# One mLSTM stage of a hybrid decoder layer: maxima differences taken from the heads' banks, keys transposed in one group, state products on column tiles

## The chip, the core and the metric

The kernel runs on one core of a Trainium2 chip. Its time is what the device needs for one launch, in microseconds (us); the figure given for a kernel is the median of several runs. One further execution is recorded by the hardware profiler, and everything read from a trace below is from that one. The engines that matter here are TensorE (PE in the profile; its weight loads are listed apart as PEld), VectorE (DVE), ScalarE (ACT), GpSimd (POOL) and the queue that issues most transfers, SyncE (SP).

## The reference

The layer is x + half a SwiGLU FFN, then x + a token mixer, then x + half a second FFN, each between two RMS norms, for 512 tokens and a width of 1024. The mixer has four HGRN2 heads and four mLSTM heads; only the mLSTM part concerns us. Cut to what is computed for one chunk of one head:

```python
b = jnp.cumsum(fc, axis=-1)                       # log forget gates, summed
a = b + m[..., None]
D = jnp.where(causal, b[..., :, None] - b[..., None, :] + ic[..., None, :], -jnp.inf)
m_t = jnp.maximum(a, jnp.max(D, axis=-1))         # running maximum
inter = jnp.exp(a - m_t)
P = jnp.einsum("bhtd,bhsd->bhts", qc, kc) * jnp.exp(D - m_t[..., None])
num = inter[..., None] * jnp.einsum("bhtd,bhdv->bhtv", qc, C) + jnp.einsum("bhts,bhsv->bhtv", P, vc)
den = inter * jnp.einsum("bhtd,bhd->bht", qc, n) + jnp.sum(P, axis=-1)
h = num / jnp.maximum(jnp.abs(den), jnp.exp(-m_t))[..., None]
w = jnp.exp(b[..., -1:] - b + ic - m_t[..., -1][..., None])
C_new = inter[..., -1][..., None, None] * C + jnp.einsum("bhs,bhsd,bhsv->bhdv", w, kc, vc)
```

Queries and keys of a head have 64 channels, values 128. All inputs and the output are float32.

## The kernel before

The kernel takes chunks of 128 tokens (NT = 4 of them), not the reference's 64, and computes the running maximum for all 512 tokens in rows before the stage below. Large products are made as three fp32r products of split operands (`mm3`, lines 196 to 200: high by high, high by low, low by high); the small products of the mixer are plain float32.

In the mixer, TensorE's queue is filled by hand. The projections of the layer (HGRN2 gates, mLSTM values and so on) are generators in `self.jobs`, and `self.fill(n)` (L1124) advances them by n steps between pieces of the recurrences. While the mLSTM stage runs, a step of a projection is one `t_mm`, three fp32r products of 128x512, seen in the trace as L198, L199, L200. These are called filling products below. Each projection holds four of the eight PSUM banks while it runs; the other four rotate among everything else. Weights of the projections lie in four places; ScalarE rounds each one (L294), VectorE subtracts for the low part (L296), and a place comes free when TensorE has read it.

The mLSTM stage is `mlstm_scores` (L1645) with `mlstm_head` (L1621) and `neg_m` (L1602):

- `self.nm2` holds the negated running maxima, heads in rows, as a high part in rows 0 to 3 and a low part in rows 32 to 35. `self.sel` is a matrix of ones and zeros with six planes; the product of plane n with `nm2` (`neg_m(n)`, L1605, 36 rows, 512 columns) spreads a row over partitions into a PSUM bank. Planes 0 to 3 spread one head over all 128 partitions. Planes 4 and 5 spread a pair: the pair's first head on partitions 0 to 63, its second on 64 to 127.
- For each head, `mlstm_head` reads the spread bank on VectorE: it adds the row term (L1628), copies the chunk ends to `nend` (L1629), clamps (L1630), then ScalarE exponentiates (L1631) and GpSimd masks (L1632). The score products (L1640) take 64 rows each; two heads of a pair alternate, one on partitions 0 to 63, one on 64 to 127. L1642 multiplies scores and decays into `pT`.
- For each pair p, `mlstm_scores` then makes the spread product of the pair's plane, copies it to SBUF (L1674), subtracts each chunk's preceding end (L1677) and exponentiates (L1680): the factor of the queries. The same for chunk ends (L1682, L1685) gives the factor of the state. Three transposes (L1691) turn the keys of the pair, L1692 multiplies them with their weights into `kw`, L1698 multiplies the queries into `qdm`; `fill(3)` follows, nine filling products.
- The states: for each chunk c of three and each pair, one product (L1706) of `kw` (128 channels of both heads) with the values and a column of ones of both heads (258 columns). Its diagonal blocks are the two heads' updates; the other two blocks are not used. VectorE copies (L1716) or accumulates (L1718) the blocks into `C`, which is zero off the diagonal blocks (memset, L1669).
- `mlstm_values` (L1745) then multiplies queries with `C` (L1753) and scores with values (L1756).

Instructions stand on TensorE's queue in the order of the program here: score products, then spread product, transposes, nine filling products, the same for the second pair, four state products, six filling products, two state products.

`sel` is built on GpSimd in `masks` (L1333 to L1343), early in the mixer; its last copy is kept as `self.selected`, behind which GpSimd issues the transfers that add up sums of later weights (L944).

Of the kernel before, what the change touches and what calls it, by code (L numbers as in the profile page):

```python
# [18 lines left out]
NT = T // P  # L19
# [9 lines left out]
NH = 4  # L29
# [94 lines left out]
class Layer:  # L124
# [1187 lines left out]
    def masks(self, mc, mb):  # L1312

        nc = self.nc

        self.mask = mb.tile([P, len(LEVELS), 2, 64], I32, name="mask")
        nc.gpsimd.memset(self.mask, 1)
        for n, c in enumerate(LEVELS):
            for odd in range(2):
                m = self.mask[:, n, odd, :].rearrange("p (b c) -> p b c", c=c)  # L1320
                for sign, base in ((1, 0), (-1, c - 1)):
                    base, step = (base + sign * (P - 1), -sign) if odd else (base, sign)
                    pat = [[-2 * c * sign, 64 // c], [0, c]]
                    nc.gpsimd.affine_select(m, m, pattern=pat, compare_op=ALU.is_ge, fill=0.0, base=base, channel_multiplier=step)
        self.eye = mb.tile([P, 2, P], I32, name="eye")
        nc.gpsimd.memset(self.eye, 1)
        for odd in range(2):
            e = self.eye[:, odd, :]
            pat, base, step = ([[1, P]], 1 - P, 1) if odd else ([[1, P]], 0, -1)
            nc.gpsimd.affine_select(e, e, pattern=pat, compare_op=ALU.is_equal, fill=0.0, base=base, channel_multiplier=step)  # L1330

        sel = mb.tile([4, 6, 2, 64], F32, tag="tmp", bufs=1, name="sel")
        nc.gpsimd.memset(sel, 1.0)  # L1333
        self.sel = mc.tile([36, 6, P], F32R, name="selr")
        nc.gpsimd.memset(self.sel.bitcast(I32), 0)
        for n in range(6):
            pat = [[0, 2], [0, 64]] if n < 4 else [[-1, 2], [0, 64]]
            base = -n if n < 4 else -2 * (n - 4)
            nc.gpsimd.affine_select(
                sel[:, n], sel[:, n], pattern=pat, compare_op=ALU.is_equal, fill=0.0, base=base, channel_multiplier=1  # L1340
            )
        for r in (0, 32):
            self.selected = nc.gpsimd.tensor_copy(self.sel[r : r + 4], sel.rearrange("p n a b -> p n (a b)"))  # L1343
    def forget_gates(self, mb):

        nc = self.nc
# [274 lines left out]
    def mlstm_head(self, h):  # L1621

        nc = self.nc
        nm = self.neg_m(h)
        nm4 = nm.rearrange("p (c t) -> p c t", c=NT)
        e = self.st("e")
        e4 = e.rearrange("p (c t) -> p c t", c=NT)
        nc.vector.tensor_tensor(e4, nm4, self.aT[:, :, h : h + 1].broadcast_to([P, NT, P]), op=ALU.add)  # L1628
        nc.vector.tensor_copy(self.nend[:, h, :].rearrange("p (c o) -> p c o", o=1), nm4[:, :, P - 1 : P])  # L1629
        nc.vector.tensor_scalar(e, e, 0.0, None, op0=ALU.min)  # L1630
        nc.scalar.activation(e, e, AF.Exp)  # L1631
        nc.gpsimd.affine_select(  # L1632
            e4, e4, pattern=[[0, NT], [1, P]], compare_op=ALU.is_ge, fill=0.0, base=0, channel_multiplier=-1
        )
        yield
        o = 64 * (h % 2)
        sc = self.ps()
        for c in range(NT):
            s = slice(c * P, (c + 1) * P)
            nc.tensor.matmul(sc[:, s], self.qk[o : o + 64, 2 + h // 2, s], self.qk[o : o + 64, h // 2, s], start=True, stop=True)  # L1640
            yield
        nc.vector.scalar_tensor_tensor(self.pT[:, h, :], sc, 0.125, e, op0=ALU.mult, op1=ALU.mult)  # L1642
        yield

    def mlstm_scores(self, mc):  # L1645

        nc = self.nc
        self.nend = mc.tile([P, NH, NT], F32, name="nend")
        self.pT = mc.tile([P, NH, T], F32, name="pT")
        H = [self.mlstm_head(h) for h in range(NH)]  # L1650
# [12 lines left out]
        nc.vector.tensor_tensor(w, self.aT, self.nend.rearrange("p h c -> p c h"), op=ALU.add)  # L1663
        nc.scalar.activation(w, w, AF.Exp)
        self.qdm = mc.tile([P, 2, 3 * P], F32, name="qdm")
        self.kw = mc.tile([P, 2, 3, P], F32, name="kw")

        self.C = mc.tile([P, 2, 3, 258], F32, name="C")
        nc.gpsimd.memset(self.C, 0.0)  # L1669
        dcs = []  # L1670
        for p in range(2):
            nm = self.neg_m(4 + p)
            ns = self.st("ns")
            nc.scalar.copy(ns, nm)  # L1674
            n4 = ns.rearrange("p (c t) -> p c t", c=NT)
            d = self.st("dq", 3 * P)
            nc.vector.tensor_tensor(  # L1677
                d.rearrange("p (c t) -> p c t", c=3), n4[:, 1:, :], n4[:, :3, P - 1 : P].broadcast_to([P, 3, P]), op=ALU.subtract
            )
            nc.scalar.activation(d, d, AF.Exp)  # L1680
            dc = self.col(2)
            nc.vector.tensor_tensor(  # L1682
                dc.rearrange("p (c o) -> p c o", o=1), n4[:, 1:3, P - 1 : P], n4[:, 0:2, P - 1 : P], op=ALU.subtract
            )
            nc.scalar.activation(dc, dc, AF.Exp)  # L1685
            dcs.append(dc)
            wp = self.col(8)[:, :6]
            nc.vector.tensor_copy(wp.rearrange("p (c a) -> p c a", a=2), w[:, :3, 2 * p : 2 * p + 2])
            pt = self.ps()
            for c in range(3):  # L1690
                nc.tensor.transpose(pt[:, c * P : (c + 1) * P], self.qk[:, 2 + p, c * P : (c + 1) * P], self.ident)  # L1691
            nc.vector.tensor_tensor(  # L1692
                self.kw[:, p].rearrange("p c (a d) -> p (c a) d", a=2),
                pt[:, : 3 * P].rearrange("p (n d) -> p n d", d=64),
                wp[:, :, None].broadcast_to([P, 6, 64]),
                op=ALU.mult,
            )
            nc.vector.scalar_tensor_tensor(self.qdm[:, p, :], self.qk[:, p, P:], 0.125, d, op0=ALU.mult, op1=ALU.mult)  # L1698
            self.fill(3)
        banks = {}  # L1700
        for c in range(3):
            for p in range(2):
                if c < 2:
                    for at in ((0, p), (1, p)) if c == 0 else ((2, p),):
                        ps = banks[at] = self.ps()
                        nc.tensor.matmul(  # L1706
                            ps[:, :258], self.kw[:, p, at[0], :],
                            self.vm[:, at[0], 2 * p : 2 * p + 2, :].rearrange("p a v -> p (a v)"), start=True, stop=True,
                        )
# [12 lines left out]

# [268 lines left out]
```

## Time and profile before

| | |
|---|---|
| median of 3 runs | 921.05 us (920.13 to 921.39) |
| profiled execution, its own time | 920.66 us |
| its span in the trace | 918.9 us |
| TensorE clock granted, mean | 0.998 |
| busy: PE, DVE, ACT, POOL | 99%, 84%, 57%, 21% of the span |
| mean busy share of the DMA engines by slice | between a tenth and nine tenths |

How to read it: the span is cut from the first to the last instruction of the trace; the launch adds 1.8 us. A row of the trace in order of time gives start, duration, engine, line, operation, output and inputs, shapes (output, input), and how many instructions were merged; in brackets, how long the engine was idle before and what ended that. A float32 product appears as two records (two passes), an fp32r product or a transpose as one. Matmuls are pipelined, so their durations overlap and the distance of two starts is what one costs. "Waits" lists who waited for whom: total, times, longest.

### The profile page before, as it was taken

To read this page: it belongs to the slowest core of one execution; us is meant where nothing else is said; L and a number is where in the kernel's file an instruction comes from. 1 tells how busy PE (TensorE), PEld (TensorE's weight loads), DVE (VectorE), ACT (ScalarE), POOL (GpSimd) and SP (SyncE) were. 2 spreads that over 40 slices of the span, in tenths; PEclk is the share of its full clock that TensorE was granted. 3 is DMA by queue.
4 is the path that set the end of the run, shared out by engine and by line. 5 is a ranking of instruction groups with operands and counts; after the bars stand their busy time and mean duration, and the time that the engine had idled before them with its cause. 6 is when DMAs were issued, how large, how long until landed. Compare 5 with 4: busy or idle time off the path is not lost.

```text
span 918.9 us, 18150 instructions
## 1 busy us (share of the span) xinstructions
PE 910.2 (99%) x7332; PEld 877.3 (95%) x7332; DVE 768.1 (84%) x1007; ACT 524.2 (57%) x753; POOL 190.6 (21%) x267
## 2 busy tenths in 40 slices
PE   9999999999999999999999999999999999999997
PEld 8999999999999999998888887899999999999997
DVE  6899988889888877799877655699899989998886
ACT  7645555547666467957634345594454545757661
POOL 2531112121111047842330310313000000010002
PEclk9999999999999999999999999999999999999999
DMA  9355879775897825699852125252354445378542
GB/s 308 84 168 131 188 186 213 188 160 139 217 286 233 247 57 140 136 204 231 186 93 79 37 92 176 81 180 74 111 161 139 138 118 160 96 229 256 170 145 93
DMA packets 123384, 145.42 MB, mean 158 GB/s; under 512 B 12066, under 2 KB 96034, under 8 KB 123300
## 3 DMA queue, kind: packets, MB, share of 16 engines
q1 hardware_dynamic: 107332, 129.05, 46.3%
q0 software_dynamic: 15680, 14.69, 11.9%
q8 instruction: 57, 0.93, 0.4%
q10 hardware_dynamic: 288, 0.52, 0.2%
q14 instruction: 27, 0.22, 0.1%
HBM read 142.14 MB, written 31.46 MB: 189 GB/s over the span
## 4 chain that ended last, share of the span: by engine, by line
PE 57%; DVE 3%; ACT 2%; DMA 1%; issue 1%; SPq 0%; DVEq 0%; POOLq 0%; POOL 0%; ACTq 0%
PE ps L619 23%; PE ps L1012 8%; PE ps L549 5%; PE ps L1004 4%; PE ps L198 4%; PE ps L200 4%; PE ps L199 4%; PE ps L560 1%; PE ps L364 1%; DMA f2sums<-in_ffn_w_out_dram 1%; PE ps L1756 0%; PE ps L1451 0%; PE ps L1729 0%; DVE w L296 0%; DVE sT L1457 0%
## 5 line engine op out<-in xcount | busy, mean ns | idle before, releaser
L294 ACT CAST w<-raw 128x1024 fp32r<-128x1024 f32 x246 | 251.0, 1027 | 189.3 <-PE ps L619 89.4
L296 DVE TENSOR_TENSOR w<-raw,w 128x1024 fp32r<-128x1024 f32 x246 | 299.8, 1222 | 30.2 <-ACT w L294 28.8
L619 PE MATMUL ps<-xq,w 128*128 128x256 f32 x2016 | 237.4, 277 | 0.0
L619 PEld LDWEIGHTS ps<-xq,w 128*128 128x128 f32 x2016 | 233.2, 188 | 0.1
L619 PE MATMUL ps<-sq,w 128*128 128x256 f32 x1512 | 178.2, 277 | 0.0
L619 PEld LDWEIGHTS ps<-sq,w 128*128 128x128 f32 x1512 | 174.8, 188 | 0.0
L310 DVE TENSOR_TENSOR raw<-raw,raw 128x1024 f32<-128x1024 f32 x72 | 89.7, 1251 | 6.3 <-DMA raw<-in_ffn_w_in_dram 4.9
L1012 PE MATMUL ps<-w,hs 128*128 128x256 f32 x672 | 80.9, 276 | 0.0
L1004 PE MATMUL ps<-w,hs 128*128 128x256 f32 x672 | 79.2, 276 | 0.0
L1012 PEld LDWEIGHTS ps<-w,hs 128*128 128x128 f32 x672 | 78.3, 188 | 0.0
L1004 PEld LDWEIGHTS ps<-w,hs 128*128 128x128 f32 x672 | 77.5, 188 | 0.0
L198 PE MATMUL ps<-w,xq 128*128 128x512 f32 x176 | 71.6, 408 | 0.2 <-DVE sT L1457 0.2
L199 PE MATMUL ps<-w,xq 128*128 128x512 f32 x176 | 68.6, 391 | 0.0
L200 PE MATMUL ps<-w,xq 128*128 128x512 f32 x176 | 68.6, 391 | 0.0
L944 POOL DMA_DIRECT2D f2sums<-in_ffn_w_out_dram x15 | 20.1, 1484 | 175.2 <-DMA f2sums<-in_ffn_w_out_dram 174.9
L549 PE MATMUL ps<-xq,w 128*128 128x256 f32 x480 | 55.7, 277 | 0.0
L549 PEld LDWEIGHTS ps<-xq,w 128*128 128x128 f32 x480 | 54.9, 188 | 0.5 <-issue 0.5
L884 ACT CAST hs<-hf 128x1024 fp32r<-128x1024 f32 x32 | 33.7, 1053 | 28.0 <-PE ps L1012 20.3
L885 DVE TENSOR_TENSOR hs<-hf,hs 128x1024 fp32r<-128x1024 f32 x32 | 39.1, 1222 | 9.0 <-ACT hs L884 8.4
L944 POOL DMA_DIRECT2D f1sums<-f1sums x26 | 21.5, 828 | 110.0 <-DMA f1sums<-in_ffn_w_out_dram 57.9
L944 POOL DMA_DIRECT2D f2sums<-f2sums x30 | 26.1, 897 | 84.0 <-DMA f2sums<-in_ffn_w_out_dram 40.2
L310 POOL TENSOR_TENSOR raw<-raw,raw 128x1024 f32<-128x1024 f32 x12 | 32.6, 2721 | 40.9 <-DVE w L296 40.7
(279 smaller groups left out, 1248.0 us busy)
## 6 DMA issues: line engine op xcount, KB each, us to landing
raw<-in_ffn_w_in_dram SPq DMA_DIRECT2D x98, 512.0 KB, 4.7
raw<-in_ffn_w_out_dram SPq DMA_DIRECT2D x44, 512.0 KB, 4.9
raw<-in_w_mix_in_dram SPq DMA_DIRECT2D x28, 512.0 KB, 4.7
raw<-f2sums SPq DMA_DIRECT2D x15, 512.0 KB, 4.6
raw<-f1sums SPq DMA_DIRECT2D x13, 512.0 KB, 6.2
raw<-in_w_mix_out_dram SPq DMA_DIRECT2D x8, 512.0 KB, 3.9
f2sums<-in_ffn_w_out_dram SPq DMA_DIRECT2D x30, 128.0 KB, 6.0
f2sums<-in_ffn_w_out_dram SPq DMA_DIRECT2D x15, 256.0 KB, 6.0
```

Of the source, the lines that this page charges most:

```text
L198: mm(ps, sh, mh, start=start, stop=False, **kw)
L199: mm(ps, sh, ml, start=False, stop=False, **kw)
L200: mm(ps, sl, mh, start=False, stop=stop, **kw)
L294: nc.scalar.copy(hi, raw)
L296: self.low = nc.vector.tensor_tensor(lo, raw, hi.bitcast(F32), op=ALU.subtract)
L310: added = (nc.vector if late else nc.gpsimd).tensor_tensor(o, o, c, op=ALU.add)
L549: mm(ps[:, u0:u1], w[:, a, k, :], self.xop(k, b, u0, u1), start=k + n + m == 0, stop=k == ND - 1 and n == 2, skip_group_check=True,)
L619: self.nc.tensor.matmul(ps[:, c], wb[b][:, k, v], left[d][:, k, :], start=first and a + n + k == 0, stop=n == 2 and k == KH - 1, skip_grou ...
L885: self.nc.vector.tensor_tensor(lo, src, hi.bitcast(F32), op=ALU.subtract)
L944: nc.gpsimd.dma_start(to[:, a:b], v, accum_op=ALU.add)
L1004: mm(out, a[kk][:, i * P : (i + 1) * P], w[:, b, kk, QUARTER * v : QUARTER * (v + 1)], start=begin and c == kk == n == 0, stop=kk == 1 and ...
L1012: mm(ps[:, QUARTER * c : QUARTER * (c + 1)], A[a][:, c], B[b], start=begin and c == n == 0, stop=n == 2, skip_group_check=True,)
```

## The change

- `sel` loses its two pair planes: four planes, four selections on GpSimd in place of six.
- `mlstm_head` also takes, from each head's own spread bank, the difference to the preceding chunk's end, on the 64 partitions where the head's queries lie, straight into `qdm`. The two spread products of pairs, the copies of their banks and their subtractions go. The exponential over both pairs' `qdm` is one instruction, as is that of the state factors, which are taken from `nend`.
- The transposes of both pairs' keys are issued together, into two banks, before the loop over pairs; `fill(3)` stays behind each pair's multiplications.
- Each state product of 128 output channels and 258 columns becomes two of 64 and 129, one per head: the first head's goes to partitions 0 to 63 of the bank, the second's to 64 to 127, both to columns 0 to 128. The blocks that were not used are no longer computed.

```diff
-        sel = mb.tile([4, 6, 2, 64], F32, tag="tmp", bufs=1, name="sel")
+        sel = mb.tile([4, NH, P], F32, tag="tmp", bufs=1, name="sel")
...
-        self.sel = mc.tile([36, 6, P], F32R, name="selr")
+        self.sel = mc.tile([36, NH, P], F32R, name="selr")
...
-        for n in range(6):
-            pat = [[0, 2], [0, 64]] if n < 4 else [[-1, 2], [0, 64]]
-            base = -n if n < 4 else -2 * (n - 4)
+        for n in range(NH):
...
@@ mlstm_head
-        nc.vector.tensor_copy(self.nend[:, h, :].rearrange("p (c o) -> p c o", o=1), nm4[:, :, P - 1 : P])
+        end = self.nend[:, h, :].rearrange("p (c o) -> p c o", o=1)
+        nc.vector.tensor_copy(end, nm4[:, :, P - 1 : P])
+        r = slice(64 * (h % 2), 64 * (h % 2) + 64)
+        d = self.qdm[r, h // 2].rearrange("p (c t) -> p c t", c=3)
+        nc.vector.tensor_tensor(d, nm4[r, 1:], end[r, :3].broadcast_to([64, 3, P]), op=ALU.subtract)
@@ mlstm_scores
-        dcs = []
+        dcs = self.col(4).rearrange("p (q c) -> p q c", q=2)
+        for a in range(2):
+            r = slice(64 * a, 64 * a + 64)
+            n = self.nend[r].rearrange("p (q a) c -> p q a c", a=2)[:, :, a, :]
+            nc.vector.tensor_tensor(dcs[r], n[:, :, 1:3], n[:, :, 0:2], op=ALU.subtract)
+        nc.scalar.activation(dcs, dcs, AF.Exp)
+        nc.scalar.activation(self.qdm, self.qdm, AF.Exp)
+        turned = [self.ps() for _ in range(2)]
+        for p, pt in enumerate(turned):
+            for c in range(3):
+                nc.tensor.transpose(pt[:, c * P : (c + 1) * P], self.qk[:, 2 + p, c * P : (c + 1) * P], self.ident)
         for p in range(2):
-            nm = self.neg_m(4 + p)
-            ns = self.st("ns")
-            nc.scalar.copy(ns, nm)
-            n4 = ns.rearrange("p (c t) -> p c t", c=NT)
-            d = self.st("dq", 3 * P)
...
-            nc.scalar.activation(d, d, AF.Exp)
-            dc = self.col(2)
...
-            nc.scalar.activation(dc, dc, AF.Exp)
-            dcs.append(dc)
...
-            pt = self.ps()
-            for c in range(3):
-                nc.tensor.transpose(pt[:, c * P : (c + 1) * P], self.qk[:, 2 + p, c * P : (c + 1) * P], self.ident)
...
-            nc.vector.scalar_tensor_tensor(self.qdm[:, p, :], self.qk[:, p, P:], 0.125, d, op0=ALU.mult, op1=ALU.mult)
+            d = self.qdm[:, p, :]
+            nc.vector.scalar_tensor_tensor(d, self.qk[:, p, P:], 0.125, d, op0=ALU.mult, op1=ALU.mult)
             self.fill(3)
...
-                        nc.tensor.matmul(
-                            ps[:, :258], self.kw[:, p, at[0], :],
-                            self.vm[:, at[0], 2 * p : 2 * p + 2, :].rearrange("p a v -> p (a v)"), start=True, stop=True,
-                        )
+                        for a in range(2):
+                            r = slice(64 * a, 64 * a + 64)
+                            nc.tensor.matmul(
+                                ps[r, :129], self.kw[:, p, at[0], r], self.vm[:, at[0], 2 * p + a, :], start=True, stop=True
+                            )
...
-                        nc.vector.tensor_copy(self.C[r, p, 0, v], ps[r, v])
+                        nc.vector.tensor_copy(self.C[r, p, 0, v], ps[r, :129])
...
-                            self.C[r, p, c, v], self.C[r, p, c - 1, v], dcs[p][r, c - 1 : c], ps[r, v], op0=ALU.mult, op1=ALU.add
+                            self.C[r, p, c, v], self.C[r, p, c - 1, v], dcs[r, p, c - 1 : c], ps[r, :129], op0=ALU.mult, op1=ALU.add
```

More of the change, by code (lines that the diff above doesn't have):

```diff
@@ L1330, in masks @@
             nc.gpsimd.affine_select(e, e, pattern=pat, compare_op=ALU.is_equal, fill=0.0, base=base, channel_multiplier=step)
-        sel = mb.tile([4, 6, 2, 64], F32, tag="tmp", bufs=1, name="sel")
+        sel = mb.tile([4, NH, P], F32, tag="tmp", bufs=1, name="sel")
         nc.gpsimd.memset(sel, 1.0)
-        self.sel = mc.tile([36, 6, P], F32R, name="selr")
+        self.sel = mc.tile([36, NH, P], F32R, name="selr")
         nc.gpsimd.memset(self.sel.bitcast(I32), 0)
-        for n in range(6):
-            pat = [[0, 2], [0, 64]] if n < 4 else [[-1, 2], [0, 64]]
-            base = -n if n < 4 else -2 * (n - 4)
+        for n in range(NH):
             nc.gpsimd.affine_select(
-                sel[:, n], sel[:, n], pattern=pat, compare_op=ALU.is_equal, fill=0.0, base=base, channel_multiplier=1
+                sel[:, n], sel[:, n], pattern=[[0, P]], compare_op=ALU.is_equal, fill=0.0, base=-n, channel_multiplier=1
             )
         for r in (0, 32):
-            self.selected = nc.gpsimd.tensor_copy(self.sel[r : r + 4], sel.rearrange("p n a b -> p n (a b)"))
+            self.selected = nc.gpsimd.tensor_copy(self.sel[r : r + 4], sel)
     def forget_gates(self, mb):
@@ L1649, in mlstm_scores @@
         self.pT = mc.tile([P, NH, T], F32, name="pT")
+        self.qdm = mc.tile([P, 2, 3 * P], F32, name="qdm")
         H = [self.mlstm_head(h) for h in range(NH)]
@@ L1664, in mlstm_scores @@
         nc.scalar.activation(w, w, AF.Exp)
-        self.qdm = mc.tile([P, 2, 3 * P], F32, name="qdm")
         self.kw = mc.tile([P, 2, 3, P], F32, name="kw")
@@ L1669, in mlstm_scores @@
         nc.gpsimd.memset(self.C, 0.0)
-        dcs = []
-        for p in range(2):
-            nm = self.neg_m(4 + p)
-            ns = self.st("ns")
-            nc.scalar.copy(ns, nm)
-            n4 = ns.rearrange("p (c t) -> p c t", c=NT)
-            d = self.st("dq", 3 * P)
-            nc.vector.tensor_tensor(
-                d.rearrange("p (c t) -> p c t", c=3), n4[:, 1:, :], n4[:, :3, P - 1 : P].broadcast_to([P, 3, P]), op=ALU.subtract
-            )
-            nc.scalar.activation(d, d, AF.Exp)
-            dc = self.col(2)
-            nc.vector.tensor_tensor(
-                dc.rearrange("p (c o) -> p c o", o=1), n4[:, 1:3, P - 1 : P], n4[:, 0:2, P - 1 : P], op=ALU.subtract
-            )
-            nc.scalar.activation(dc, dc, AF.Exp)
-            dcs.append(dc)
+        dcs = self.col(4).rearrange("p (q c) -> p q c", q=2)
[9 more added lines that the diff above has]
+                nc.tensor.transpose(pt[:, c * P : (c + 1) * P], self.qk[:, 2 + p, c * P : (c + 1) * P], self.ident)
+        for p in range(2):
             wp = self.col(8)[:, :6]
             nc.vector.tensor_copy(wp.rearrange("p (c a) -> p c a", a=2), w[:, :3, 2 * p : 2 * p + 2])
-            pt = self.ps()
-            for c in range(3):
-                nc.tensor.transpose(pt[:, c * P : (c + 1) * P], self.qk[:, 2 + p, c * P : (c + 1) * P], self.ident)
             nc.vector.tensor_tensor(
                 self.kw[:, p].rearrange("p c (a d) -> p (c a) d", a=2),
-                pt[:, : 3 * P].rearrange("p (n d) -> p n d", d=64),
+                turned[p][:, : 3 * P].rearrange("p (n d) -> p n d", d=64),
                 wp[:, :, None].broadcast_to([P, 6, 64]),
@@ L1705, in mlstm_scores @@
                         ps = banks[at] = self.ps()
-                        nc.tensor.matmul(
-                            ps[:, :258], self.kw[:, p, at[0], :],
-                            self.vm[:, at[0], 2 * p : 2 * p + 2, :].rearrange("p a v -> p (a v)"), start=True, stop=True,
-                        )
+                        for a in range(2):
[3 more added lines that the diff above has]
+                            )
             for p in range(2):
```

## The prediction, made before the changed kernel ran

> **What bounds the kernel now.** I read the page first (engine shares, slices), then TensorE's own waits, then the instructions of TensorE in order of time around the change.
>
> ```profile
> span 918.9 us, 18150 instructions
> ...
> PE 910.2 (99%) x7332; PEld 877.3 (95%) x7332; DVE 768.1 (84%) x1007; ACT 524.2 (57%) x753; POOL 190.6 (21%) x267
> PE ps L194 <- POOL ones L172: 1.2, 1, 1.2
> PE ps L364 <- DVE xn L754: 0.2, 1, 0.2
> PE ps L619 <- ACT xq L384: 0.2, 1, 0.2
> PE ps L198 <- DVE sT L1457: 0.2, 1, 0.2
> ```
>
> TensorE is busy 99% of the span, and its whole list of waits comes to 1.8 us, 1.2 of them at the very start. Nothing after the mixer makes it wait: the last entry, on sT, stands ahead of the stage that changes. So a TensorE nanosecond taken out of this stage should move everything behind it forward, and work of other engines costs nothing until TensorE has to wait for it. The change is therefore priced in TensorE start times. The stage starts with the burst of score products (L1640), the fifth spread product (L1605) and the first three transposes (L1691):
>
> ```profile
> 481.45 0.39 PE L200 MATMUL ps<-w,xq 128*128 128x512 f32 x1
> 481.77 1.16 PE L1640 MATMUL ps<-qk 64*128 64x128 f32 x16
> 482.86 0.50 PE L198 MATMUL ps<-w,xq 128*128 128x512 f32 x1
> 483.20 0.39 PE L199 MATMUL ps<-w,xq 128*128 128x512 f32 x1
> ...
> 486.62 0.39 PE L199 MATMUL ps<-w,xq 128*128 128x512 f32 x1
> 486.85 0.39 PE L200 MATMUL ps<-w,xq 128*128 128x512 f32 x1
> 487.17 1.16 PE L1640 MATMUL ps<-qk 64*128 64x128 f32 x16
> 488.08 0.48 PE L1605 MATMUL ps<-nm,selr 36*128 36x512 f32 x1
> 488.49 0.55 PE L1691 MATMUL ps<-ident,qk 128*128 128x128 f32 x3
> 488.79 0.48 PE L198 MATMUL ps<-w,xq 128*128 128x512 f32 x1
> 489.11 0.40 PE L199 MATMUL ps<-w,xq 128*128 128x512 f32 x1
> ...
> 490.71 0.39 PE L200 MATMUL ps<-w,xq 128*128 128x512 f32 x1
> 491.03 0.50 PE L1605 MATMUL ps<-nm,selr 36*128 36x512 f32 x1
> 491.46 0.55 PE L1691 MATMUL ps<-ident,qk 128*128 128x128 f32 x3
> 491.76 0.48 PE L198 MATMUL ps<-w,xq 128*128 128x512 f32 x1
> 492.08 0.40 PE L199 MATMUL ps<-w,xq 128*128 128x512 f32 x1
> ...
> 493.69 0.39 PE L200 MATMUL ps<-w,xq 128*128 128x512 f32 x1
> 493.92 1.90 PE L1706 MATMUL ps<-vm,kw 128*128 128x258 f32 x8
> 495.46 0.58 PE L198 MATMUL ps<-w,xq 128*128 128x512 f32 x1
> 495.89 0.39 PE L199 MATMUL ps<-w,xq 128*128 128x512 f32 x1
> ```
>
> Read start to start: the durations overlap, since matmuls are pipelined. A filling product takes 486.85 - 486.62 = 0.23 us. To price a burst I take the time from the filling product ahead of it (L200) to the second one behind it (L199) and subtract two filling products, 0.46. So the score burst costs 483.20 - 481.45 - 0.46 = 1.29; score burst, spread product and three transposes cost 489.11 - 486.85 - 0.46 = 1.80; the second spread product with its transposes 492.08 - 490.71 - 0.46 = 0.91; the first state burst 495.89 - 493.69 - 0.46 = 1.74.
>
> Two things are inside these numbers. The state burst enters without a pause (493.92 - 493.69 is the usual 0.23), and its 8 records, 4 fp32 products of two passes, take 0.22 each for 258 columns. The score burst, which uses 64 rows at a time, enters late (481.77 - 481.45 = 0.32) and leaves late (483.20 - 482.86 = 0.34), and its 16 records of 128 columns take (488.08 - 487.17)/16 = 0.057 each. For the same columns on the full array the chain of waits has
>
> ```profile
> 469.24 2.68 PE ps L1515 x24
> ```
>
> that is 2.68/24 = 0.112 a record. So the two heads of the score burst, on rows 0 to 63 and 64 to 127, run side by side: eight pairs of 0.112 are 0.90, and the remaining 1.29 - 0.90 = 0.39 is what entering and leaving the other array shape costs.
>
> **The change, part by part.** *Spread products and transposes.* Both products with the pair rows of the selector go; six transposes stand together. In the first group the spread product takes 488.49 - 488.08 = 0.41 with the way back to the full shape; that way back (half of 0.39, 0.20) stays, so 0.41 - 0.20 = 0.21 goes. Three transposes come in, at 0.11 each (488.79 - 488.49 = 0.30, a tenth each, to 0.13 with the late filling product behind): +0.33. The second group, 0.91, goes whole. Sum: -0.21 + 0.33 - 0.91 = -0.79 us. Bounds: with transposes of 0.13 and all of the 0.39 staying, -0.02 + 0.39 - 0.91 = -0.54; with transposes of 0.10, -0.82.
>
> *State products.* Four products of 128 columns out and 258 streamed become eight of 64 out and 129 streamed (then two become four), one per head, in the lower or upper half of the array's columns and of the bank. No row here has column halves. The nearest is the score burst: also 16 records, also two halves that alternate, 128 against 129 columns streamed. Taking its price, the first burst costs 1.29 instead of 1.74: -0.45. The second has half the records: 0.45 + 0.39 = 0.84 against half of 1.74, 0.87: -0.03. Sum -0.48. From below: halves side by side and no cost of changing shape, 12 pairs of 0.112 = 1.34 against 2.61, -1.27. From above: no overlap and two changes of shape, 24 x 0.112 + 0.78 = 3.47, +0.86, and more if loads show (rivals). I take -0.48, since the score burst is the same pattern of records.
>
> The Trainium skill, TensorE: Matmul & The Clock Gate, Part 3 (Packing small matmuls), gives 2.38x for three column tiles, near what it gives for row tiles; the 0.057 above agrees for rows, and no run so far shows columns. The Trainium skill, TensorEngine Tiling (Array Packing), Key Properties, says that a change of tiling mode drains the array, for columns too: this speaks against the change, since the old state burst needed no such change. By it the sum is -0.48 for this part, without it -1.27.
>
> *VectorE and ScalarE.* Four subtractions out of the heads' banks replace two of 128x384 behind copies; a 128x768 exponential replaces two copies and two exponentials of 384.
>
> ```profile
> 477.22 1.69 DVE L1630 TENSOR_SCALAR e<-e 128x512 f32<-128x512 f32 x1
> 477.23 1.40 POOL L1669 MEMSET C<- 128x1548 f32 x1
> ...
> 484.14 1.27 DVE L1642 SCALAR_TENSOR_TENSOR pT<-ps,e 128x512 f32<-128x512 f32 x2
> 485.34 0.21 DVE L1688 COPY col<-w 128x6 f32<-128x6 f32 x2
> 485.64 1.22 DVE L296 TENSOR_TENSOR w<-raw,w 128x1024 fp32r<-128x1024 f32 x1
> 488.43 1.29 DVE L1642 SCALAR_TENSOR_TENSOR pT<-ps,e 128x512 f32<-128x512 f32 x2 [1.57 <-PE ps L1640]
> 489.63 0.55 DVE L1677 TENSOR_TENSOR dq<-ns 128x384 f32<-128x384 f32 x1
> ...
> 492.05 0.56 DVE L1692 TENSOR_TENSOR kw<-ps,col 128x384 f32<-128x384 f32 x1 [0.65 <-PE ps L1691]
> ```
>
> At 0.55 each (384 elements a lane, half the lanes) the four cost 2.2 us between 477 and 484. The first hides where the clamp L1630 took 1.69 beside GpSimd's 1.40 memset of C; about 1.65 remain. They run into VectorE's idle 1.57 ahead of 488.43, so the second pair of pT slips by some 0.1 to 0.6; then two subtractions (1.1) and two small ones are gone, and both key products (L1692) can end near 492. The state burst would start at 493.92 - 0.79 = 493.13. So some 1 us of cover is left; if it were gone, TensorE would wait for kw by what is missing.
>
> The heads' banks are held 0.55 longer each, and the six transposes need two banks at about 488.3, the ones that the first pair of pT gives back. That pair ended at 485.41 and would end 1.65 later, at 487.1, or at 488.3 if the split L296 (1.22) gets ahead of it. Either is in time, the second barely; I price it at 0, with 0.4 as the bound. The exponential over qdm waits for all four subtractions, and behind it on ScalarE are the casts of weights (L294); their readers on TensorE appear nowhere in its waits and the kernel holds four weight places, so a cast 1 us late has cover of a whole weight. The products of qdm (L1698) move ahead of the state burst and end earlier. No DMA is added or moved; SP's queue is untouched.
>
> *Selector.* Two of six selections and a third of two fills and two copies leave GpSimd:
>
> ```profile
> 375.50 2.50 POOL L1339 TENSOR_SCALAR_AFFINE_SELECT sel<-sel 4x128 f32<-4x128 f32 x6
> 378.06 2.05 POOL L1343 CAST selr<-sel 4x768 fp32r<-4x768 f32 x2
> ```
>
> About 0.6 + 0.7 us from these rows; the accumulating transfers queued behind them on GpSimd start that much earlier. What lies before 451 us can give TensorE at most the 0.2 that it waited for sT: 0.
>
> **Sum.** -0.79 - 0.48 = -1.27 us. The profiled execution took 920.66 for a span of 918.9; less 1.27 that is 919.4. It lay 0.4 below the median of the runs shown, 921.05, on which the forecast is 919.8.
>
> **Rivals.** *No cost of the column shape* (forecast's mechanism, cheaper): for it, halves of the columns need no other rows; against it, the two late steps at the score burst. -0.79 - 1.27 = -2.06: 919.0.
>
> *Column halves don't overlap* (the change doesn't do what it says): both halves read the same 128 partitions of kw and vm, where the row pairs read different ones. Then -0.79 + 0.86 = +0.07: 921.1.
>
> *Weight loads show* (slower): 24 loads instead of 12, each into rows that the other half is still streaming through. A load takes
>
> ```profile
> L1706 PEld LDWEIGHTS ps<-vm,kw x12: 187/189/193, 493.7 to 497.5; 128*128 128x128 f32 x12
> ```
>
> 0.189, hidden today, with one load for 0.22 us of streaming. With x us of each load exposed and no overlap the time is +0.07 + 24x: slower by over 0.2% from x = 0.074, 923.4 at half a load (0.094), 925.7 at a whole one. For it: there is no row of two halves sharing rows; against it: the full-array records of L1515 hide their load in 0.112. The Trainium skill, in the same Part 3, says that a load overlaps running matmuls only where the row group differs, or into the background buffer; its load time by columns, in Part 2 (LDWEIGHTS), gives an estimate of 0.053 for 64, and with it 922.4.
>
> **How the numbers follow.** A change of 0.2%, 1.84 us, is about what a measurement of this kernel tells from none. Forecast (919.8) 0.46, of which 0.12 lies beyond that bound, since its own width, from the transposes, the banks and the scatter of runs (920.13 to 921.39), is about 1 us to each side (918.8 to 920.8); no shape cost (919.0) 0.22, of which 0.19; no overlap (921.1) 0.14, nearly all within; loads (923.4 or more) 0.18, of which 0.15 slower. Faster 0.31, same 0.53, slower 0.16. The range goes from 917.9 (the cheapest case and one scatter of runs below it) to 923.4, which leaves out half of the loads' rival and a little at the bottom.
>
> **What would show it.** Right: two L1605 groups instead of three, with six L1691 in one burst; the time from the filling product ahead of the first L1706 burst to the second behind it near 1.75 instead of 2.20, its pairs starting a few ns apart at 0.11 us a pair; no new wait in TensorE's list. Wrong: pairs a full 0.11 apart (no overlap), gaps of a load between them (loads), the first filling product entering and leaving at 0.23 (no shape cost), or an entry of L1691 on DVE pT or of L1706 on DVE kw.

## The result, and the profile after

The changed kernel takes **928.33 us** (median of 6 runs, 928.09 to 928.68) against 920.73 for the kernel before (6 runs, 919.80 to 921.39). The ratio is 1.0083, with a 95% interval of 1.0070 to 1.0096: slower by 7.6 us, where 919.8 and a range of 917.9 to 923.4 were forecast. The profiled execution took 928.09, for a span of 926.4.

The page's span and busy shares, and TensorE's list of waits, of the changed kernel:

```profile
span 926.4 us, 18163 instructions
...
PE 917.1 (99%) x7342; PEld 885.0 (96%) x7342; DVE 766.7 (83%) x1009; ACT 523.6 (57%) x749; POOL 188.5 (20%) x265
PE ps L194 <- POOL ones L172: 1.2, 1, 1.2
PE ps L364 <- DVE xn L754: 0.5, 1, 0.5
PE ps L619 <- ACT xq L384: 0.4, 1, 0.4
PE ps L198 <- DVE sT L1456: 0.3, 1, 0.3
```

There is no new wait: the list has the same four entries, 2.4 us instead of 1.8. TensorE waits 0.6 us more; above all it is *busy* longer, 917.1 us instead of 910.2. So the next thing to read is which instructions are busier. TensorE's groups by line, of the kernel before (line, engine, operation, moving operand and weights, shapes, count, busy us, mean ns, idle us before):

```profile
L619 PE MATMUL ps<-xq,w 128*128 128x256 f32 x2016 | 237.4, 277 | 0.0
L619 PE MATMUL ps<-sq,w 128*128 128x256 f32 x1512 | 178.2, 277 | 0.0
L1004 PE MATMUL ps<-w,hs 128*128 128x256 f32 x672 | 79.2, 276 | 0.0
L549 PE MATMUL ps<-xq,w 128*128 128x256 f32 x480 | 55.7, 277 | 0.0
```

and of the kernel after:

```profile
L619 PE MATMUL ps<-xq,w 128*128 128x256 f32 x2016 | 237.5, 277 | 0.0
L619 PE MATMUL ps<-sq,w 128*128 128x256 f32 x1512 | 184.2, 279 | 0.0
L1004 PE MATMUL ps<-w,hs 128*128 128x256 f32 x672 | 79.6, 277 | 0.0
L549 PE MATMUL ps<-xq,w 128*128 128x256 f32 x480 | 57.5, 282 | 0.0
```

None of these lines is in the mLSTM stage, and none is touched by the diff: L619, L1004 and L549 are fp32r products of 256 columns, in the two FFNs and between the first of them and the recurrences. The counts are the same; 1512 products of `sq` on `w` take 6.0 us more and 480 products of L549 take 1.8 more, while 2016 products of `xq` on `w` on the very same line take what they took. These two groups and L1004's 0.4 make 8.2 us, the waits 0.6 more; the difference of the spans is 7.5, so some 1.3 must have been gained somewhere.

How a product is slower is seen in order of time. The second FFN, before, and then the same place after (start, duration):

```profile
647.43 2.88 PE L619 MATMUL ps<-xq,w 128*128 128x256 f32 x24
650.15 5.60 PE L619 MATMUL ps<-sq,w 128*128 128x256 f32 x48
655.59 11.10 PE L619 MATMUL ps<-xq,w 128*128 128x256 f32 x96
```

```profile
651.48 2.89 PE L619 MATMUL ps<-xq,w 128*128 128x256 f32 x24
654.21 5.82 PE L619 MATMUL ps<-sq,w 128*128 128x256 f32 x48
659.86 8.38 PE L619 MATMUL ps<-xq,w 128*128 128x256 f32 x72
```

Start to start, the 48 products of `sq` take (655.59 - 650.15)/48 = 0.113 us each before and (659.86 - 654.21)/48 = 0.118 after. The 24 of `xq` just ahead take 0.113 and 0.114. Same line, same shape, same engine, no gap: only the operand differs. A stretch of the first FFN in the view of windows says the same (busy us and count of PE, PEld, DVE, ACT, POOL; granted clock; DMA share; GB/s), before and then after:

```profile
51.00:223.00 172.00, 172.00 (x1509) 172.00 (x1508) 155.04 (x169) 94.55 (x120) 34.46 (x31) 1.00 0.72 177
```

```profile
51.00:223.00 172.00, 172.00 (x1488) 172.00 (x1488) 152.87 (x164) 92.27 (x116) 33.65 (x30) 1.00 0.71 175
```

TensorE is busy for all of the 172 us in both and the granted clock is 1.00 in both, yet 21 products fewer are started. It is not the clock, and not a wait.

The stage that changed, in order of time, after:

```profile
491.46 0.39 PE L200 MATMUL ps<-w,xq 128*128 128x512 f32 x1
491.78 1.16 PE L1643 MATMUL ps<-qk 64*128 64x128 f32 x16
492.87 0.87 PE L1683 MATMUL ps<-ident,qk 128*128 128x128 f32 x6
493.50 0.48 PE L198 MATMUL ps<-w,xq 128*128 128x512 f32 x1
493.81 0.39 PE L199 MATMUL ps<-w,xq 128*128 128x512 f32 x1
...
497.46 0.39 PE L200 MATMUL ps<-w,xq 128*128 128x512 f32 x1
497.78 1.10 PE L1704 MATMUL ps<-vm,kw 128*64 128x129 f32 x16
498.81 0.50 PE L198 MATMUL ps<-w,xq 128*128 128x512 f32 x1
499.15 0.39 PE L199 MATMUL ps<-w,xq 128*128 128x512 f32 x1
...
500.08 0.40 PE L200 MATMUL ps<-w,xq 128*128 128x512 f32 x1
500.41 0.66 PE L1704 MATMUL ps<-vm,kw 128*64 128x129 f32 x8
501.00 0.50 PE L198 MATMUL ps<-w,xq 128*128 128x512 f32 x1
501.34 0.40 PE L199 MATMUL ps<-w,xq 128*128 128x512 f32 x1
```

By the method of the prediction (first filling product to the second one behind, less 0.46): scores with six transposes 493.81 - 491.46 - 0.46 = 1.89, where 1.80 + 0.91 stood before; first state burst 499.15 - 497.46 - 0.46 = 1.23 instead of 1.74; second 501.34 - 500.08 - 0.46 = 0.80 instead of 0.88 (498.15 - 496.81 - 0.46, in the trace of the kernel before). The stage gained 0.82 + 0.51 + 0.08 = **1.41 us**, and -1.27 was forecast. The matmuls of the two traces, matched one by one, say it in one line: the changed kernel is 4.61 us late when it enters the stage (481.22 against 485.83), 3.19 late when it leaves it (498.15 against 501.34), and 7.45 late at the end. What was lost, was lost ahead of the stage and behind it.

### The profile page after: what moved, and what is told of

It is laid out like the page before. It is cut to its first block, busy times and chain, and to the rows that moved or that the text cites. A ratio compares the mean times of both kernels' runs of the same rounds, so it can differ in the third digit from the quotient of the medians.

```text
span 926.4 us, 18163 instructions
## 1 busy us (share of the span) xinstructions
PE 917.1 (99%) x7342; PEld 885.0 (96%) x7342; DVE 766.7 (83%) x1009; ACT 523.6 (57%) x749; POOL 188.5 (20%) x265
## 4 chain that ended last, share of the span: by engine, by line
PE 56%; DVE 3%; ACT 2%; DMA 1%; issue 1%; SPq 0%; DVEq 0%; POOLq 0%; POOL 0%; ACTq 0%
PE ps L619 23%; PE ps L1012 8%; PE ps L549 5%; PE ps L1004 4%; PE ps L198 4%; PE ps L200 4%; PE ps L199 4%; PE ps L560 1%; PE ps L364 1%; DMA f2sums<-in_ffn_w_out_dram 1%; DVE w L296 1%; DVE qk L1618 0%; ACT w L294 0%; PE ps L1753 0%; PE ps L1450 0%
## 5 line engine op out<-in xcount | busy, mean ns | idle before, releaser
L619 PE MATMUL ps<-xq,w 128*128 128x256 f32 x2016 | 237.5, 277 | 0.0
L619 PEld LDWEIGHTS ps<-xq,w 128*128 128x128 f32 x2016 | 233.6, 188 | 0.0
L619 PE MATMUL ps<-sq,w 128*128 128x256 f32 x1512 | 184.2, 279 | 0.0
L619 PEld LDWEIGHTS ps<-sq,w 128*128 128x128 f32 x1512 | 180.5, 188 | 0.0
L1012 PE MATMUL ps<-w,hs 128*128 128x256 f32 x672 | 80.9, 276 | 0.0
L1004 PE MATMUL ps<-w,hs 128*128 128x256 f32 x672 | 79.6, 277 | 0.0
L1012 PEld LDWEIGHTS ps<-w,hs 128*128 128x128 f32 x672 | 78.3, 188 | 0.0
L1004 PEld LDWEIGHTS ps<-w,hs 128*128 128x128 f32 x672 | 77.9, 188 | 0.0
L549 PE MATMUL ps<-xq,w 128*128 128x256 f32 x480 | 57.5, 282 | 0.0
L549 PEld LDWEIGHTS ps<-xq,w 128*128 128x128 f32 x480 | 56.6, 189 | 0.5 <-issue 0.5
L198 PEld LDWEIGHTS ps<-w,xq 128*128 128x128 f32 x176 | 33.1, 188 | 8.6 <-issue 1.3
```

Of the source, the lines that this page charges most:

```text
L198: mm(ps, sh, mh, start=start, stop=False, **kw)
L549: mm(ps[:, u0:u1], w[:, a, k, :], self.xop(k, b, u0, u1), start=k + n + m == 0, stop=k == ND - 1 and n == 2, skip_group_check=True,)
L619: self.nc.tensor.matmul(ps[:, c], wb[b][:, k, v], left[d][:, k, :], start=first and a + n + k == 0, stop=n == 2 and k == KH - 1, skip_grou ...
L1004: mm(out, a[kk][:, i * P : (i + 1) * P], w[:, b, kk, QUARTER * v : QUARTER * (v + 1)], start=begin and c == kk == n == 0, stop=kk == 1 and ...
L1012: mm(ps[:, QUARTER * c : QUARTER * (c + 1)], A[a][:, c], B[b], start=begin and c == n == 0, stop=n == 2, skip_group_check=True,)
```

## What could slow untouched products

Before the stage the two programs differ in little on the other engines: two selections on GpSimd, and the place of tiles in SBUF. `dc = self.col(2)` was the only use of its tag, and the diff removes it. Its four places of 32 bytes a partition go with it, and all that is allocated behind them lies 128 bytes lower. By the allocator's addresses in the two built kernels:

```
bytes in a partition     before                     after
xq (places 1, 2, 3)      33440, 41632, 49824        the same
w                        87136 on                   the same
sq and hs                180960, 189664, 198368     180832, 189536, 198240
```

So the slow group is the one whose moving operand moved against its weights. **Theory A**: the pace of such a product depends on the distance of the two operands' addresses, modulo some power of two; after the shift that distance, moving operand less weights, is 64 instead of 192 modulo 256. **Rival B**: the new order of the mixer's work (the early exponential, the bursts) slows TensorE through other engines' traffic. **Rival C**: the smaller selector shifts GpSimd's transfers of sums.

## The experiments

**Put the 128 bytes back.** The changed kernel with four places of the same size in the same pool:

```diff
         dcs = self.col(4).rearrange("p (q c) -> p q c", q=2)
+        nc.gpsimd.memset(self.sp.tile([P, 2], F32, tag="pad", bufs=4, name="pad"), 0.0)
```

> The changed kernel with one unused tile of four small columns (128 bytes a partition) put back where the old pair columns lay, so that every later SBUF tile stands at its old address. If the shift of 128 bytes slows the FFN products (layout theory): L619 sq,w records 0.113 us apart again instead of 0.118, time about 919.5, 1.3 below before (ratio 0.9986). If the new instructions themselves cost the 7.6 us (rival: column tiles or the longer VectorE chain): still about 928.

Measured: 919.16 us (11 runs), ratio 0.9984 [0.9975, 0.9993], span 917.0. The group that had lost most, in this kernel:

```profile
L619 PE MATMUL ps<-sq,w 128*128 128x256 f32 x1512 | 177.5, 276 | 0.0
```

L549 is back at 55.7 too. The whole loss is gone with one line that computes nothing. B falls: the mixer's order is that of the changed kernel.

**Shift the kernel before.** None of the change, only the column taken from another tag, so that tag `col2` has no use:

```diff
-            dc = self.col(2)
+            dc = self.col(4)[:, :2]
```

> The kernel before, with the two small columns of the state factor taken from the tag of four columns, so that only the layout changes: all later tiles 128 bytes lower, no instruction different. Layout theory: 920.7 + 7.6 + 1.3 = about 929.6, with L619 sq,w at 0.118. Rival (the instructions cost it): 920.7, nothing changes.

Measured: 929.81 us, ratio 1.0102 [1.0088, 1.0115], span 928.4. The slow groups are those of the changed kernel to the digit, L549 with its 57.5 and L1004 with its 79.6 among them:

```profile
L619 PE MATMUL ps<-sq,w 128*128 128x256 f32 x1512 | 184.2, 279 | 0.0
```

The shift alone makes the old kernel slow. By the medians the change is worth 929.81 - 928.33 = 1.5 us at the shifted addresses (from two sets of runs), and 920.41 - 919.16 = 1.25 at the old ones (920.41 is the kernel before, measured beside the first experiment). The spans of the profiled executions say 928.4 - 926.4 = 2.0 and 918.9 - 917.0 = 1.9, but these are single executions: 0.63 of the 2.0 is there at 30 us already, where both programs still do the same.

**The selector's size.** The first kernel with the selector allocated with its six planes again, four of them used:

```diff
-        self.sel = mc.tile([36, NH, P], F32R, name="selr")
+        self.sel = mc.tile([36, 6, P], F32R, name="selr")[:, :NH, :]
```

> As the first, and the selector tile keeps its old size too, so that the mixer's own tiles also stand where they stood. If the 128 bytes alone explain the L549 records going from 0.113 to 0.118 (1.7 us of the loss): the same time as the first run within 0.5 us. If the shorter selector tile does it: the first run is about 1.7 us slower than this one.

Measured: 919.12 us, ratio 0.9987 [0.9978, 0.9996]: the same as without. The place that the selector takes costs nothing (it is 1024 bytes smaller, a multiple of 256). As the four-plane selector runs at full pace here and in the first experiment, C falls too.

**More than was there.** A pad of 384 bytes, so that the tiles lie 256 bytes *above* where the kernel before has them:

```diff
+        nc.gpsimd.memset(self.sp.tile([P, 96], F32, tag="pad", bufs=1, name="pad"), 0.0)
```

> The changed kernel with 384 bytes put in: later tiles 256 bytes above their old places instead of at them. If what counts is the distance of a product's two operands modulo 256 bytes (192 before, 64 after): as fast as the first run, 919.5. If the absolute addresses, or the distance to the old place, count: slower than the first run by several us.

Measured: 918.77 us, ratio 0.9983 [0.9974, 0.9992]; `sq` on `w` 177.7 us. The old place itself does not matter; a place 256 bytes from it is as good.

**The stage's two parts.** The first experiment with the full-width state products of the kernel before:

```diff
-                        for a in range(2):
-                            r = slice(64 * a, 64 * a + 64)
-                            nc.tensor.matmul(
-                                ps[r, :129], self.kw[:, p, at[0], r], self.vm[:, at[0], 2 * p + a, :], start=True, stop=True
-                            )
+                        nc.tensor.matmul(
+                            ps[:, :258], self.kw[:, p, at[0], :],
+                            self.vm[:, at[0], 2 * p : 2 * p + 2, :].rearrange("p a v -> p (a v)"), start=True, stop=True,
+                        )
```

> The first experiment (old addresses) with the state products back to one of 128 columns by 258 per pair. From the starts in the changed kernel's trace the two column-tile bursts cost 1.23 + 0.80 = 2.03 us with the change of shape, the two full-width bursts before 1.74 + 0.88 = 2.62. If column halves run side by side: this is 0.6 slower than the first experiment, about 919.8, and faster than before by 0.7 from the spread products alone. If the halves gain nothing in the whole: 919.2, as the first.

Measured: 919.67 us, ratio 0.9990 [0.9982, 0.9999], 0.5 more than with column tiles. The span, 918.0, is 1.0 longer, but 0.27 of that is there at 30 us, where both programs still do the same. The intervals of the two kernels overlap, so the clocked times alone don't separate them; the bursts do. In order of time, first with the full width (this experiment), then with column tiles (the first experiment):

```profile
492.55 0.39 PE L200 MATMUL ps<-w,xq 128*128 128x512 f32 x1
492.77 1.90 PE L1703 MATMUL ps<-vm,kw 128*128 128x258 f32 x8
494.32 0.58 PE L198 MATMUL ps<-w,xq 128*128 128x512 f32 x1
494.75 0.39 PE L199 MATMUL ps<-w,xq 128*128 128x512 f32 x1
```

```profile
492.28 0.39 PE L200 MATMUL ps<-w,xq 128*128 128x512 f32 x1
492.60 1.10 PE L1705 MATMUL ps<-vm,kw 128*64 128x129 f32 x16
493.63 0.50 PE L198 MATMUL ps<-w,xq 128*128 128x512 f32 x1
493.97 0.39 PE L199 MATMUL ps<-w,xq 128*128 128x512 f32 x1
```

494.75 - 492.55 - 0.46 = 1.74 against 493.97 - 492.28 - 0.46 = 1.23: the column tiles are worth 0.51 in the first burst, and the first of them enters 0.32 behind the filling product, where the full-width one enters at 0.22.

**Five other distances.** The same pad with other sizes, n floats in one place:

```diff
+        nc.gpsimd.memset(self.sp.tile([P, n], F32, tag="pad", bufs=1, name="pad"), 0.0)
```

64 bytes (n = 16):

> The changed kernel with 64 bytes put in: later tiles 64 below their old places, so the moving operand sq stands 128 bytes past the weights w modulo 256, where it stood 192 (fast) before and 64 (slow) in the changed kernel. If 192 alone is good: slow, about 928. If 64 alone is bad: about 919.2.

192 bytes (n = 48):

> The changed kernel with 192 bytes put in: later tiles 64 above their old places, distance of sq to w 0 modulo 256. If 192 alone is good: slow, about 928. If 64 alone is bad: about 919.2.

32 bytes (n = 8):

> The changed kernel with 32 bytes put in: distance of sq to w 96 modulo 256, between the slow 64 and the untried 128. If lines of 64 bytes count: as the changed kernel, 928. If the slow place is narrower than 64 bytes: faster than 925.

96 bytes (n = 24):

> The changed kernel with 96 bytes put in: distance of sq to w 160 modulo 256, between the slow 128 and the fast 192. If the fast place is 192 alone: slower than 925. If it is a stretch that begins above 128: about 919.

160 bytes (n = 40):

> The changed kernel with 160 bytes put in: distance of sq to w 224 modulo 256, between the fast 192 and the slow 0. If the fast place is 192 alone: slower than 925. If it is a stretch up to 256: about 919, or below if the best place is not the old one.

Measured, with the distances (moving operand less weights, modulo 256) from the built kernels and the mean from start to start of the group's products from the traces, in ns:

| kernel | `sq` on `w`: distance, pace | `w` on `hs` (L1012): distance, pace | median us | ratio and interval |
|---|---|---|---|---|
| before | 192, 113.8 | 192, 113.3 | 920.73 | |
| after | 64, 117.8 | 64, 113.3 | 928.33 | 1.0083 [1.0070, 1.0096] |
| pad 32 | 96, 119.6 | 32, 116.7 | 934.24 | 1.0152 [1.0138, 1.0165] |
| pad 64 | 128, 118.7 | 0, 120.0 | 943.67 | 1.0252 [1.0238, 1.0266] |
| pad 96 | 160, 117.4 | 224, 118.2 | 936.12 | 1.0170 [1.0155, 1.0185] |
| pad 128 | 192, 113.3 | 192, 113.3 | 919.16 | 0.9984 [0.9975, 0.9993] |
| pad 160 | 224, 118.1 | 160, 120.1 | 937.49 | 1.0182 [1.0165, 1.0199] |
| pad 192 | 0, 119.5 | 128, 118.3 | 936.75 | 1.0179 [1.0163, 1.0194] |

Pads 64, 96, 160 and 192 are slow, as expected if 192 alone is good, but by more than the 928 that was written for two of them; pad 32 fits neither of its two expectations. The groups of the slowest, pad 64, show that another joins in (80.9 us before):

```profile
L619 PE MATMUL ps<-sq,w 128*128 128x256 f32 x1512 | 185.7, 281 | 0.0
L1012 PE MATMUL ps<-w,hs 128*128 128x256 f32 x672 | 85.3, 283 | 0.0
```

Nor are these two all: in the same trace the products of `w` on `hs` at L1004 take 83.5 us instead of 79.2, and the 600 products of `w` on `xq` and on `once` at L1004 and L1012, which lie at 192 in every kernel, take 80.5 instead of 77.8. So a product's own distance is not the whole rule; the last section comes back to that.

Seven of the eight multiples of 32 were tried for each group, and only 192 is fast for both. Of the values tried, the kernel before stood at the one that suits both. The changed kernel got off lightly: at 64, `w` on `hs` keeps its pace.

**Distance or address?** Of the operands of these products the pads move only `sq` and `hs`, so an effect of their own addresses would look the same. Two kernels move `w` and `xq` as well, by widening a constant tile in front of them all. The first experiment with everything 64 bytes higher:

```diff
-        self.nhalf = self.cp.tile([P, 8], F32, name="nhalf")
+        self.nhalf = self.cp.tile([P, 24], F32, name="nhalf")[:, :8]
```

> This is the kernel of e1_pad128 with a constant tile in front of everything widened by 64 bytes, so that the weights (w), xq, sq and hs all lie 64 bytes higher and every distance between them is as in the kernel before (sq - w 192, w - hs 192, modulo 256). If the pace of the products follows from the distance between the two operands: as e1_pad128, 919.2 us (918 to 920.5), sq on w 177.5 us busy. If it follows from the address of the moved tile by itself (sq 64 higher modulo 256, an address at which p2_pad192 was slow): sq on w some 186 us, w on hs some 84, the whole 930 or more. A kernel between 922 and 928 would speak for neither.

Measured: 918.53 us, ratio 0.9982 [0.9973, 0.9992], `sq` on `w` 177.5. The address of `sq` is now the one that was slow with pad 192, and the kernel is fast. And the changed kernel with everything 128 bytes higher (40 floats in place of 24):

> This is the changed kernel with the same constant tile widened by 128 bytes: sq and hs are back at the addresses that they have in the kernel before, but w and xq lie 128 bytes higher, so that the distances are those of the changed kernel (sq - w 64). By the distance: as the changed kernel, 928.3 us (927.3 to 929.3), sq on w 184.2 us busy, L549 57.5. By the address of sq and hs alone: 919.2 us, sq on w 177.5 and L549 55.7.

Measured: 926.62 us, ratio 1.0067 [1.0050, 1.0084], a little below the range expected by distance and far from the 919.2 expected by address:

```profile
L619 PE MATMUL ps<-sq,w 128*128 128x256 f32 x1512 | 184.2, 279 | 0.0
...
L549 PE MATMUL ps<-xq,w 128*128 128x256 f32 x480 | 55.7, 277 | 0.0
```

`sq` is back at its old address and still slow: it is the distance. But neither theory had L549 right: its distances are those of the changed kernel and its 1.8 us are gone, which is about the difference of 928.33 and 926.62. So 6.0 us of the loss follow from the distance, and the 1.8 of L549 don't follow from its own.

## Why the prediction was wrong, step by step

**The stage was read right.** Transposes and spread products: -0.79 forecast, -0.82 measured. State products: -0.48 forecast, -0.59 measured. The two halves of the columns run side by side (16 records in one burst of 1.23 us, pairs at 0.11), and changing the array's shape costs as it does for rows: the burst enters 497.78 - 497.46 = 0.32 behind the filling product and the filling product leaves at 499.15 - 498.81 = 0.34, where 0.23 is usual. That settles three rivals: *no cost of the column shape*, *halves don't overlap* and *loads show* all fall. The last by the loads' own row, of the changed kernel (24 loads, ns least, median and most, first and last start):

```profile
L1704 PEld LDWEIGHTS ps<-vm,kw x24: 133/136/137, 497.8 to 500.7; 128*64 128x64 f32 x24
```

Loads of 0.136 us come every 0.055 (16 records from the burst's start to the last one's, (1.10 - 0.27)/15) and no gap shows between them. That holds although a load takes 0.136, not the 0.053 that the prediction estimated. The rule of the Trainium skill, TensorE: Matmul & The Clock Gate, Part 3 (The mechanism), that a load overlaps running matmuls only where the row group differs, would have made this rival true, unless the load goes into the background buffer, which the same section allows; these halves share all 128 rows, and the trace shows no exposed load. The drain on a change of mode that the Trainium skill, TensorEngine Tiling (Array Packing), Key Properties, states agrees with the 0.32 and 0.34.

**The zeros of the other engines held.** On VectorE the second pair of pT didn't slip, and both key products were done 2.5 us ahead of the state burst, where 1 us of cover had been forecast:

```profile
493.05 1.28 DVE L1645 SCALAR_TENSOR_TENSOR pT<-ps,e 128x512 f32<-128x512 f32 x2
494.25 1.01 DVE L1687 TENSOR_TENSOR kw<-ps,col 128x384 f32<-128x384 f32 x2
```

(494.25 + 1.01 = 495.26 against 497.78.) Banks, casts and selector cost nothing that a wait shows.

**The step that failed** is the frame of the sum: "What lies before 451 us can give TensorE at most the 0.2 that it waited for sT", and that a saving in the stage "should move everything behind it forward". Both take for granted that TensorE's time outside the stage is its waits, and that products which nobody edits cost what they cost. They don't: 4.6 us were lost ahead of the stage and 7.45 - 3.19 = 4.26 behind it, and only 0.6 of that as waits. The forecast gave a slower kernel a chance through weight loads alone, and that rival fell; the loss came by a way that it did not have. The term missing from the sum is one tile with a tag of its own. The prediction priced `dc`'s instructions and not its place. It is that place that did it, shown by taking it away from the old kernel and by giving it back to the new one; and 6.0 us of the loss came by the distance of operands, shown by moving everything together. With the place given back the change does what was forecast: 919.16 us is 1.25 below the 920.41 of the kernel before measured beside it, and 1.27 was forecast. That the two agree so closely is luck, since the runs of that kernel go from 917.93 to 919.87.

**What stays open.** Why 192 is fast and the others slow isn't known. Nor is what decides the pace that L549 starts with; the last section has what the traces show of it.

## What to carry to other kernels

Where an engine is busy 99% of the span, compare the time per instruction of the groups that were *not* edited before looking for a cause in those that were; a group whose count is the same and whose busy time moved is the place to look. An edit that adds or drops a tile moves every tile allocated behind it, so test a change once with the old layout padded back in: here one idle line turned +0.83% into -0.16%. And the layout itself is a thing to tune: the same program ran between 918.5 and 943.7 us by nothing but pads, more than this change could ever give.

## What the runs showed of the hardware

**Distance of operands.** In these kernels TensorE's fp32r products of `sq` on `w` and of `w` on `hs`, 256 columns wide, run at 113.3 ns where moving operand and weights lie 192 bytes apart modulo 256 (113.8 for one group of the kernel before), and at 117 to 120 ns at the other multiples of 32 that were tried, with `w` on `hs` at 64 (113.3) as the exception. In the kernel before, without any pad, 152 of the 2016 products of `xq` on `w` lie at distance 0; they take 117.7 on the mean, and 1820 of the others, which lie at 192, 113.9. The filling products of 512 columns lie at distance 0 in every kernel and run at 0.227 us, twice 113.5 ns; no other distance was tried at that width. The Trainium skill, SBUF — State Buffer, section "SBUF: two separate sides", has TensorE never waiting on anyone there. That is said of other engines, and these rows don't speak against it; they show a TensorE that loses 4% to where its own two operands lie.

**A pace that carries over.** Products at one and the same distance can run at either pace. After 226 us in the changed kernel:

```profile
226.49 5.82 PE L1004 MATMUL ps<-w,hs 128*128 128x256 f32 x48
232.14 2.88 PE L619 MATMUL ps<-xq,w 128*128 128x256 f32 x24
234.86 5.60 PE L1004 MATMUL ps<-w,hs 128*128 128x256 f32 x48
240.30 1.52 PE L1012 MATMUL ps<-w,xq 128*128 128x256 f32 x12
```

The first 48 of `w` on `hs` follow slow products of `sq` and take (232.14 - 226.49)/48 = 0.118; after 24 fast ones of `xq` the next 48, at the same distance of 64, take (240.30 - 234.86)/48 = 0.113. L549 is the other case: all its 480 products lie at 192 in every kernel. They took 55.7 us in the kernel before, with pads of 128, 192 and 384 and in both kernels that moved everything, 57.5 in the changed kernel and in the shifted old one, and 56.2, 57.0, 56.2 and 57.8 with pads of 32, 96, 160 and 64. They stand in four stretches of 288, 18, 126 and 48, with other products between, and each stretch keeps one pace. The longest, in the changed kernel and then in the changed kernel with everything 128 bytes higher:

```profile
355.37 34.08 PE L549 MATMUL ps<-xq,w 128*128 128x256 f32 x288
```

```profile
355.31 32.80 PE L549 MATMUL ps<-xq,w 128*128 128x256 f32 x288
```

The 126 took 15.41 and 14.87 us in the same two kernels, the 18 the other way round, 2.30 and 2.37. So here a pace is taken up where a stretch begins and is held to its end, and L549's 1.8 us are its two longest stretches at the slow pace. The kernel before has a slow stretch too: from 51 to 69 us its products of `sq`, at distance 192, run at 0.118, which the first experiment's don't. It begins just behind two late steps at 47.3 us, of 0.16 and 0.23 where 0.113 is usual. The first experiment goes from 0.29 us behind at 50 us to 0.44 ahead at 69, is 0.59 ahead when it enters the stage and 1.91 when it leaves, and so its span is 1.9 us shorter, of which the stage gives 1.3. What decides which pace a stretch takes up was not tried.
